# The turn from attention to the MLP in an encoder layer: the last heads' store by another queue, blocks begun a row sooner, a product emitted ahead of casts

## The chip, the cores and the metric

The kernel runs on one core of one Trainium2 chip. TensorE (PE) multiplies matrices, VectorE (DVE), ScalarE (ACT) and GpSimd (POOL) work on vectors, and SyncE (SP) issues most of the DMAs. The metric is the device time of one execution in microseconds (us), as the median of the runs.

## What is computed

One encoder layer on a sequence of 2048 tokens with 1024 features, in float32: a mixer of two groups of eight heads, and a squared-ReLU MLP. Both sub-layers have an RMS norm and a scale, shift and gate drawn from a vector c.

```python
h = rmsnorm(x, g_norm1) * (1.0 + sc1) + sh1
q_sb, k_sb, v_sb, q_ca, k_ca, v_ca = split(h @ w_in)
o_sb = stick_breaking_attention(q_sb, k_sb, v_sb)            # 8 heads, causal
o_ca = chunked_relpos_attention(norm(q_ca), norm(k_ca), v_ca, rel_bias)
x = x + gt1 * (concat(o_sb, o_ca) @ w_o)                     # output projection
h = rmsnorm(x, g_norm2) * (1.0 + sc2) + sh2
x = x + gt2 * (square(relu(h @ w1)) @ w2)                    # MLP, 4096 hidden
```

## The kernel before

**Numbers in two parts.** A float32 operand is split into a rounded part and a remainder (`split`, line 141: ScalarE casts the rounded part, VectorE or GpSimd subtracts to get the remainder, "low part" below). A product of two such operands is three matmuls (`mm3`): high by high, high by low, low by high.

**Four blocks of tokens, worked from the last to the first.** The sequence (stored reversed) is cut into four blocks g of 512 tokens. The heads are walked for g = 2 and 3, then 1, then 0, and the output projection of a block is filled in between the attention matmuls of the next. The last head pair of block 0 is thus the end of the attention. `keep` (line 798) splits the finished output o of a pair of heads into the tile os, subtracting on GpSimd, and stores it in scr_m. The choice of the queue for that store is one line (802): ScalarE's for the very last unit, GpSimd's for the other late pairs of block 0, else SyncE's.

**The turn.** When the attention is over, five of the eight rows of block 1's output projection are still left or in work (`left`, the matmuls named po; weights ow; residuals xr and txr). `row` (line 2114) emits a row to its end and the first matmul of the next one, which is where the next row's weight and residual loads are emitted. Between the rows the code emits loads and work of the MLP (`steps[0].fetch` loads the mixer's outputs of block 0, opm; `some(k, n)` emits piece n of block k, below).

Then comes a list of steps, which the loop in line 2150 emits one by one: each iteration first prepares operands of steps ahead (as many as eight tiles allow), then emits the jobs due at that step, then runs the step. The first eight are `Mixed` (line 1992): the output projection of block 0, one row each (matmuls pso; the weights still resident are ow, the others wo; residuals cxr), in the order of rows 5, 6, 7, 0 to 4. After them come the `First` steps (line 1587): the first dense layer of the MLP for the half mb = 1 of the tokens, that is blocks 2 and 3 of scr_x, by a scheme of seven products of halves instead of eight, in the order 1, 5, 6, 3, 7, 2, 4. Product 1 has a PSUM bank ps of its own; when it is done, ScalarE copies that bank to seed the bank ps_s of product 6 (lines 1643 to 1645), which products 7 and 4 go on with. The weights of products 1 and 5 are split into a tile of their own (opr) before the step; those of 6, 3, 7, 2 and 4 (opw) go into the eight buffers that held opm.

**The right-hand blocks.** The seven products need seven combinations of the normed activations, in four blocks k of 128 features (`right_blocks`, line 1503). Piece 0 loads four tiles y of scr_x (named ty for k = 0, cy for k = 1 to 3); piece 1 multiplies them by the norm's factor r on VectorE, scales and shifts them on ScalarE and casts the first three high parts; pieces 2 and 3 make the low parts, the differences and the other high parts h, going to and fro between VectorE and ScalarE. The second to fourth blocks are emitted in pieces beside the Mixed steps (`pieces`, line 2143). This half's blocks are what the change calls the second half's.

**What sets the order.** Each engine runs its instructions in the order in which the code emits them (`Ordered`, line 34; in the profile all such instructions have line 42). So a SyncE DMA that waits holds up all DMAs behind it. The DMAs of SyncE and ScalarE together take eight counters of landings in turn (DMAHW0 to DMAHW7), and GpSimd's take others (DMASW): a DMA that gets a counter waits until the DMA that had it eight places earlier has landed.

Of the kernel before, what the change touches and what calls it, by code (L numbers as in the profile page):

```python
# [24 lines left out]
KT = D // P  # L25
# [54 lines left out]
def encoder_kernel(ctx, tc, xs, c, g1, g2, w_in, w_first, w_rest, gqk, bias, w_o, w1, w2, w_ada, b_ada, out):  # L80
    nc = tc.nc
    act, dve, pool, sp = nc.scalar, nc.vector, nc.gpsimd, nc.sync
# [58 lines left out]
    def split(hi, lo, src, lo_eng=None):  # L141
        act.copy(hi, src)
        (lo_eng or dve).tensor_tensor(lo, src, hi.bitcast(F32), op=ALU.subtract)
# [100 lines left out]
    if True:  # L244
# [251 lines left out]
        act, dve, pool = (Ordered(tc, e) for e in (act, dve, pool))  # L496
# [161 lines left out]
        sp = osp  # L658
# [78 lines left out]
    if True:  # L737
# [7 lines left out]
        sp = nc.sync  # L745
# [28 lines left out]
        def finish(u):  # L774
            r = (u.h % 2) * HD
            q = HD - r
            if u.h % 2 == 0:
                pend["o", u.g] = op.tile([P, TB], F32, tag="o", name=f"o{u.nm}")
            o = pend["o", u.g]
            tmp = op.tile([P, TB], F32, tag="otmp", name=f"otmp{u.nm}")  # L780
            rows = slice(r, r + HD)
            act.copy(tmp[rows, :], u.acc[q : q + HD, :])

            def rest():
                act.copy(o[rows, :], u.acc[rows, :])
                soon.append(add)

            def add():
                pool.tensor_tensor(o[rows, :], o[rows, :], tmp[rows, :], op=ALU.add)
                if u.h % 2:  # L790
                    wait({3: 5, 0: 2}.get(u.g, 3), lambda: (urgent if u.g > 1 else heavy).append(lambda: keep(u, o)))

            urgent.append(rest)
# [4 lines left out]
        def keep(u, o):  # L798

            os = fp.tile([P, 2, TB], F32R, tag="st", name=f"os{u.nm}")  # L800
            split(os[:, 0, :], os[:, 1, :], o, pool)
            q = act if u is units[-1] else pool if u.ca and u.g == 0 else sp
            q.dma_start(scr_m[u.g, u.ca * 4 + u.h // 2], os.bitcast(F32))
            if u.ca and u.h == NH - 1 and u.g > 0:
                filler.append(Filler(outproj, u.g))
# [434 lines left out]
        units = []  # L1240
# [70 lines left out]
        def force(f):  # L1311

            got = next(f.gen, None)
            if callable(got):
                got()
            return None if got is None else callable(got)
# [41 lines left out]
        for i in range(len(steps) + LAG):  # L1358
# [31 lines left out]
            n = len(urgent) + len(heavy)  # L1390
# [4 lines left out]
            if i + 1 < len(steps):  # L1395
                u, st = steps[i + 1]
# [8 lines left out]
    sp = osp  # L1405
# [21 lines left out]
    if True:  # L1427
# [610 lines left out]
        for mb in (1, 0):  # L2038
# [22 lines left out]
            if mb:  # L2061
                norm2(1, begin + 18)
                norm2(0, begin + 48)
                for k in range(HK):
                    begins = end + 6 * k
                    pieces = right_blocks(0, k, kept if k % 2 else temp)
# [41 lines left out]
        def some(k, *ns):  # L2108
            for n in ns:
                blocks[k][n]()  # L2110
# [3 lines left out]
        def row():  # L2114

            while force(left) is False:
                pass
            while len(stores) > 2:
                stores.pop(0)()
            return force(left)  # L2120

        steps[0].fetch(0, KT // 2)
        row()
        row()
        some(0, 0)
        steps[0].fetch(KT // 2, KT - 2)
        row()
        some(0, 1)
        steps[0].fetch(KT - 2, KT)
        row()  # L2130
        some(0, 2)
        some(1, 0)
        while row() is not None:
            pass
        while stores:
# [4 lines left out]
            del resident[n]  # L2140
        for m in range(LEFT):
            steps[m].load()
        pieces = ((0, 3), (1, 1)), ((1, 2), (2, 0)), ((1, 3), (2, 1)), ((2, 2), (3, 0)), ((2, 3), (3, 1)), ((3, 2),), ((3, 3),)
        for n, now in enumerate(pieces):
            for k, m in now:
                at(n, lambda k=k, m=m: some(k, m))
# [1 line left out]
        ahead = iter(steps[1:])  # L2148
        nxt = next(ahead)
        for n, s in enumerate(steps):  # L2150
            while nxt is not None and ready - used + nxt.tiles <= 8 and nxt.ready():
                nxt.prepare()
                ready += nxt.tiles
                nxt = next(ahead, None)
            for m in (0, 1) if n == 0 else (n + 1,):
                if m < KT:
                    steps[m].load_row()
            for job in jobs.get(n, ()):
                job()
            if n == KT - 1:  # L2160
                firsts = spare.tile([P, 2, 2, TB], F32R, tag="r8", name="opr")
                steps[KT].prepare(firsts[:, 0])
                steps[KT].fetch(0)
                steps[KT + 1].prepare(firsts[:, 1])
                for m in range(1, 4):
                    steps[KT].fetch(m)
            s.run()
            used += s.frees
            later.tick()
        later.flush()  # L2170
# [42 lines left out]
```

## Time and profile before

| | us |
|---|---|
| median of 3 runs | 2512.6 |
| the runs | 2511.39 to 2512.66 |
| the profiled execution | 2509.76 |
| its span in the profile | 2508.1 |
| TensorE busy | 2497.6 |
| VectorE busy | 2028.4 |
| ScalarE busy | 1527.0 |
| GpSimd busy | 788.5 |

The turn lies at about 1266 to 1354 us of the span. In the rows of the profile a name like po<-fx,ow says that the instruction writes po and reads fx and ow; x96 is a count; "SPq" and "ACTq" are DMAs issued by SyncE and ScalarE. Bracketed text says how long the engine was idle before the instruction and what is thought to have ended that. Matmul durations overlap, since TensorE is pipelined. The granted TensorE clock was 0.999 over the run.

### The profile page before, as it was taken

The page shows a single profiled execution, that of the slowest core. Times are in us where ns is not written, and L with a number is a line of the kernel's source. Part 1 is how long each engine was busy: PE and PEld are TensorE (multiplying, and loading weights), DVE is VectorE, ACT ScalarE, POOL GpSimd, SP SyncE. Part 2 cuts the span into 40 slices and gives each one's busy share as a digit, 9 for nine tenths or more (in the row PEclk, how much of TensorE's full clock was granted, in tenths as well). Part 3 has the DMA queues.
Part 4 walks back from the last instruction along what each step waited for, and adds up shares of the span by engine and source line. Part 5 has one row for each costly group of instructions (what it writes and reads, how often), then busy time and mean ns, then how long its engine had stood idle before and what let it go on. Part 6 is the DMA issues. An engine that isn't in the chain of part 4 may idle for free.

```text
span 2508.1 us, 39516 instructions
## 1 busy us (share of the span) xinstructions
PE 2497.6 (100%) x12364; PEld 2094.6 (84%) x12364; DVE 2028.4 (81%) x3572; ACT 1527.0 (61%) x2928; POOL 788.5 (31%) x1174
## 2 busy tenths in 40 slices
PE   9999999999999999999999999999999999999999
PEld 8888888888888888888887888888888888888887
DVE  7656776897789888999868777779877759799998
ACT  6333434778876687666755555567555546577765
POOL 4330154777776677776720000000000000010100
PEclk9999999999999999999999999999999999999999
DMA  9879978789888788866786878996998996988982
GB/s 359 331 297 362 356 274 290 231 262 310 268 262 263 235 249 269 271 193 214 220 327 243 299 284 304 333 355 196 326 326 269 316 365 260 319 248 282 305 279 84
DMA packets 296114, 704.71 MB, mean 281 GB/s; under 512 B 32096, under 2 KB 88672, under 8 KB 284256
## 3 DMA queue, kind: packets, MB, share of 16 engines
q1 hardware_dynamic: 287552, 684.22, 79.1%
q0 software_dynamic: 6768, 13.11, 2.9%
q10 hardware_dynamic: 1584, 4.85, 0.5%
q8 instruction: 98, 1.61, 0.3%
q14 instruction: 112, 0.92, 0.1%
HBM read 473.99 MB, written 228.07 MB: 280 GB/s over the span
## 4 chain that ended last, share of the span: by engine, by line
PE 93%; DVE 3%; ACT 1%; DMA 1%; issue 1%; POOL 0%; SPq 0%; DVEq 0%; ACTq 0%; POOLq 0%
PE ps L42 29%; PE ps_s L42 17%; PE pt L42 11%; PE acc L42 7%; PE wt L42 7%; PE pf L42 6%; PE z L42 5%; PE po L42 4%; PE pq L42 3%; PE cz L42 2%; PE ct L42 1%; DMA opm<-scr_m 1%; PE px L42 1%; DVE h L42 0%; DVE p L42 0%
## 5 line engine op out<-in xcount | busy, mean ns | idle before, releaser
L42 ACT CAST wth<-wt 128x512 fp32r<-128x512 f32 (+3 forms) x544 | 257.8, 484 | 173.3 <-PE wt L42 160.7
L42 PE MATMUL ps<-h,opw 128*128 128x512 f32 x1512 | 358.6, 389 | 0.0
L42 POOL TENSOR_TENSOR b<-p 128x512 f32<-128x512 f32 (+1 forms) x320 | 292.5, 914 | 153.2 <-DVE p L42 94.3
L42 DVE TENSOR_TENSOR wtl<-wt,wth 128x512 fp32r<-128x512 f32 (+3 forms) x544 | 291.3, 547 | 60.4 <-ACT wth L42 56.0
L42 PEld LDWEIGHTS ps<-h,opw 128*128 128x128 f32 x1512 | 283.6, 188 | 58.9
L42 PE MATMUL pt<-w,ht 128*128 128x512 f32 x1248 | 288.0, 391 | 0.0
L42 PE MATMUL ps_s<-h,opw 128*128 128x512 f32 x1152 | 277.8, 390 | 1.0 <-ACT ps_s L42 1.0
L42 PEld LDWEIGHTS pt<-w,ht 128*128 128x128 f32 x1248 | 232.9, 188 | 47.5
L42 DVE TENSOR_TENSOR_SCAN p<-z,p,zero 128x512 f32<-128x512 f32 x192 | 245.2, 1279 | 18.6 <-ACT z L42 14.8
L42 PEld LDWEIGHTS ps_s<-h,opw 128*128 128x128 f32 x1152 | 215.6, 188 | 47.6 <-ACT ps_s L42 1.4
L42 ACT CAST opr<-r 128x512 fp32r<-128x512 f32 x280 | 174.3, 623 | 118.2 <-PE ps L42 66.4
L42 PE MATMUL acc<-wth,v 128*128 128x512 f32 (+3 forms) x544 | 221.3, 410 | 0.0
L42 PE MATMUL ps<-opr,ol 128*128 128x512 f32 x960 | 220.3, 389 | 0.0
L42 PEld LDWEIGHTS ps<-opr,ol 128*128 128x128 f32 x960 | 180.1, 188 | 37.8 <-DVE opr L42 0.4
L42 ACT ACTIVATE z<-z 128x512 f32<-128x512 f32 (+1 forms) x320 | 166.6, 521 | 52.7 <-PE z L42 49.9
L42 DVE TENSOR_TENSOR opr<-r,opr 128x512 fp32r<-128x512 f32 x280 | 185.5, 683 | 13.8 <-ACT opr L42 12.7
L42 PE MATMUL acc<-wtl,v 128*128 128x512 f32 (+3 forms) x544 | 185.6, 347 | 0.0
L42 PE MATMUL z<-k,q 128*128 128x512 f32 (+3 forms) x640 | 182.8, 367 | 0.7 <-DVE p L42 0.7
L42 POOL DMA_DIRECT2D scr_x<-txu x12 | 10.4, 868 | 544.2 <-DMA scr_x<-txo 314.9
L42 PE MATMUL ps<-oph,opv 128*128 128x512 f32 x768 | 174.9, 389 | 0.2 <-DVE txo L42 0.2
L42 PE MATMUL wt<-ident,b 128*128 128x128 f32 x1088 | 170.7, 272 | 0.4 <-DVE p L42 0.4
L42 PEld LDWEIGHTS ps<-oph,opv 128*128 128x128 f32 x768 | 144.1, 188 | 30.5 <-DVE txo L42 0.6
(238 smaller groups left out, 5064.7 us busy)
## 6 DMA issues: line engine op xcount, KB each, us to landing
r<-scr_hid SPq DMA_DIRECT2D x80, 512.0 KB, 7.5
q<-scr_q SPq DMA_DIRECT2D x128, 256.0 KB, 5.3
w<-in_w_dram SPq DMA_DIRECT2D x64, 512.0 KB, 5.8
k<-scr_k SPq DMA_DIRECT2D x240, 128.0 KB, 4.5
v<-scr_v SPq DMA_DIRECT2D x120, 256.0 KB, 4.3
wa<-in_w_ada_dram SPq DMA_DIRECT2D x48, 512.0 KB, 6.1
ow<-scr_wo SPq DMA_DIRECT2D x24, 1024.0 KB, 5.7
l<-scr_t SPq DMA_DIRECT2D x20, 1024.0 KB, 8.6
```

The lines of the kernel that those rows point to most:

```text
L42: return lambda *x, **y: self.tc.keep_in_program_order(f(*x, **y))
```

## The change

Three edits. The store of the last head pair goes by GpSimd's queue, as those of the other late pairs of block 0 do. At the turn every piece of a right-hand block is emitted a row sooner: the loads of block 0 after the first row that is left instead of the second, and so on, so that two pieces more are emitted within the rows of block 1 and the list beside the Mixed steps begins at what was its second entry. And the first `First` step is emitted before the operands of the steps ahead are prepared (`if n == KT: s.run()`, KT is 8), not after.

```diff
-            q = act if u is units[-1] else pool if u.ca and u.g == 0 else sp
+            q = pool if u.ca and u.g == 0 else sp
...
         steps[0].fetch(0, KT // 2)
         row()
+        some(0, 0)
         row()
-        some(0, 0)
         steps[0].fetch(KT // 2, KT - 2)
+        some(0, 1)
         row()
-        some(0, 1)
         steps[0].fetch(KT - 2, KT)
-        row()
         some(0, 2)
         some(1, 0)
+        row()
+        some(0, 3)
+        some(1, 1)
         while row() is not None:
             pass
...
-        pieces = ((0, 3), (1, 1)), ((1, 2), (2, 0)), ((1, 3), (2, 1)), ((2, 2), (3, 0)), ((2, 3), (3, 1)), ((3, 2),), ((3, 3),)
+        pieces = ((1, 2), (2, 0)), ((1, 3), (2, 1)), ((2, 2), (3, 0)), ((2, 3), (3, 1)), ((3, 2),), ((3, 3),)
...
         for n, s in enumerate(steps):
+            if n == KT:
+                s.run()
             while nxt is not None and ready - used + nxt.tiles <= 8 and nxt.ready():
                 nxt.prepare()
...
-            s.run()
+            if n != KT:
+                s.run()
```

SyncE's queue at the turn, before: the numbers behind a name tell one row or part of it (ow_7 is the weight of row 7, opm_4 the output of head pair 4), and the waits are in brackets.

```order
L42 DMA ow_6_16972<-scr_wo_236 128x2048 [waits DMAHW5_49,PE_49]
L42 DMA txr_5_16974<-in_xs_dram 128x512 [waits DMAHW6_49,Pool_49]
L42 DMA ow_7_17002<-scr_wo_237 128x2048 [waits DMAHW7_49,PE_49]
L42 DMA txr_6_17004<-in_xs_dram 128x512 [waits DMAHW0_49]
L42 DMA ty_0_11_17008<-scr_x_0_216 128x512 [waits DMAHW1_49]
L42 DMA ty_0_12_17010<-scr_x_0_208 128x512 [waits DMAHW2_49]
L42 DMA ty_0_21_17012<-scr_x_4_220 128x512 [waits DMAHW3_49]
L42 DMA ty_0_22_17014<-scr_x_4_212 128x512 [waits DMAHW4_49]
L42 DMA opm_4_17016<-scr_m_4_164 128x1024 [waits DMAHW5_49,DMASW0_49]
```

The counter DMAHW0 that txr_6 waits for is the one that ScalarE's store of the last heads has taken. The same place after the change:

```order
L42 DMA ow_6_16972<-scr_wo_236 128x2048 [waits DMAHW4_49,PE_49]
L42 DMA txr_5_16974<-in_xs_dram 128x512 [waits DMAHW5_49,Pool_49]
L42 DMA ty_0_11_16978<-scr_x_0_216 128x512 [waits DMAHW6_49]
L42 DMA ty_0_12_16980<-scr_x_0_208 128x512 [waits DMAHW7_49]
L42 DMA ty_0_21_16982<-scr_x_4_220 128x512 [waits DMAHW0_49]
L42 DMA ty_0_22_16984<-scr_x_4_212 128x512 [waits DMAHW1_49]
L42 DMA ow_7_17010<-scr_wo_237 128x2048 [waits DMAHW2_49,PE_49]
L42 DMA txr_6_17012<-in_xs_dram 128x512 [waits DMAHW3_49]
L42 DMA opm_4_17016<-scr_m_4_164 128x1024 [waits DMAHW4_49,DMASW0_49]
```

The four loads of ty have moved ahead of ow_7 and txr_6. The counters are one lower, since ScalarE's store takes none; opm_7 now waits for GpSimd's counter DMASW3 instead.

ScalarE's queue at the first dense products, before (opr and opw are the high parts of the weights; ps_0_1_s is the bank ps_s):

```order
L42 CAST opr<-ts_0_1_5_17492 128x512 [waits DVE_49]
L42 CAST opw_0_6_17528<-ts_0_1_6_17496 128x512 [waits DMAHW1_49,DVE_49,PE_49]
L42 CAST opw_0_3_17531<-ts_0_1_3_17498 128x512 [waits DMAHW2_49,DVE_49,PE_49]
L42 CAST opw_0_7_17534<-w_1_0_17445 128x512 [waits DMAHW4_49,DVE_49,PE_49]
L42 CAST opw_0_2_17537<-w_1_0_17445 128x512 [waits PE_49]
L42 CAST opw_0_4_17540<-w_1_0_17445 128x512 [waits DMAHW5_49,PE_49]
L42 COPY ps_0_1_s<-ps_0_1_17543 128x512 [waits PE_49]
```

The copy stands last here, behind the five casts. The same place after the change:

```order
L42 CAST opr<-ts_0_1_5_17492 128x512 [waits DVE_49]
L42 COPY ps_0_1_s<-ps_0_1_17528 128x512 [waits PE_49]
L42 CAST opw_0_6_17543<-ts_0_1_6_17496 128x512 [waits DMAHW0_49,DVE_49]
L42 CAST opw_0_3_17546<-ts_0_1_3_17498 128x512 [waits DMAHW1_49,DVE_49]
L42 CAST opw_0_7_17549<-w_1_0_17455 128x512 [waits DMAHW3_49,DVE_49]
L42 CAST opw_0_2_17552<-w_1_0_17455 128x512
L42 CAST opw_0_4_17555<-w_1_0_17455 128x512 [waits DMAHW4_49]
```

The copy that seeds ps_s has moved ahead of the five casts. On VectorE each block's products, differences and low parts stand one residual (txr or cxr) sooner than before. On TensorE the order of the matmuls is the same.

## The prediction

> **What bounds the kernel now.** I read the page first, the engines' busy times (its part 1).
>
> ```profile
> PE 2497.6 (100%) x12364; PEld 2094.6 (84%) x12364; DVE 2028.4 (81%) x3572; ACT 1527.0 (61%) x2928; POOL 788.5 (31%) x1174
> ```
>
> TensorE is busy in 2497.6 of 2508.1 us. So the change can win only time in which TensorE stands still around the turn, and that has to be measured in that stage. The next view is TensorE's timeline there: start, time, instruction, count, and in brackets the idle time before it.
>
> ```profile
> 1266.80 22.00 PE L42 MATMUL po<-fx,ow 128*128 128x512 f32 x96
> 1288.64 16.73 PE L42 MATMUL pso<-opm,ow 128*128 128x512 f32 x72
> 1305.20 27.36 PE L42 MATMUL pso<-opm,wo 128*128 128x512 f32 x120
> 1332.40 0.61 PE L42 MATMUL ps<-h,opr 128*128 128x512 f32 x2
> 1333.20 5.28 PE L42 MATMUL ps<-h,opr 128*128 128x512 f32 x22 [0.18 <-DVE opr L42]
> 1339.44 3.06 PE L42 MATMUL ps_s<-h,opw 128*128 128x512 f32 x12 [0.96 <-ACT ps_s L42]
> ...
> 1345.19 3.02 PE L42 MATMUL ps_s<-h,opw 128*128 128x512 f32 x12
> ...
> 1350.78 2.92 PE L42 MATMUL ps_s<-h,opw 128*128 128x512 f32 x12
> 1353.54 5.60 PE L42 MATMUL ps<-h,opw 128*128 128x512 f32 x24
> 1358.98 2.88 PE L42 MATMUL ps_s<-h,opw 128*128 128x512 f32 x12
> ```
>
> The durations hold a pipeline's drain, so I count from start to start. The last two rows give the pace without waits: 24 matmuls in 5.44 us, 0.2267 us each. Against that pace, the 96 po matmuls took 21.84 for 21.76 us (0.08 lost); the 72 pso matmuls on ow 16.56 for 16.32 (0.24); the 120 on wo 27.20 for 27.20 (nothing); the first two matmuls of the first dense product 0.80 for 0.45 (0.35); from there to ps_s 6.24 for 4.99 (1.25); the four products from 1339.44 to 1350.78 took 11.34 for 10.88 (0.46), the next one lost 0.04. In all **2.42 us**: that is all the turn can give back, less than 0.1% of the kernel.
>
> Next, who holds those matmuls up. ScalarE's timeline:
>
> ```profile
> 1274.04 0.33 ACTq L42 DMA_DIRECT2D scr_m<-os  x1
> ...
> 1333.78 0.62 ACT L42 CAST opr<-ts 128x512 fp32r<-128x512 f32 x1 [2.10 <-DVE ts L42]
> 1335.81 1.35 ACT L42 CAST opw<-ts 128x512 fp32r<-128x512 f32 x2 [1.41 <-PE ps L42]
> 1337.14 1.66 ACT L42 CAST opw<-w 128x512 fp32r<-128x512 f32 x3
> 1338.82 0.57 ACT L42 COPY ps_s<-ps 128x512 f32<-128x512 f32 x1
> ...
> 1344.56 0.58 ACT L42 COPY cp<-ps_s 128x512 f32<-128x512 f32 x1
> ```
>
> VectorE's:
>
> ```profile
> 1283.67 0.69 DVE L42 TENSOR_TENSOR ty<-ty,r 128x512 f32<-128x512 f32 x1 [4.91 <-DMA ty<-scr_x]
> ...
> 1330.43 1.46 DVE L42 TENSOR_TENSOR h<-cy,h 128x512 fp32r<-128x512 f32 x2
> 1331.80 0.74 DVE L42 SCALAR_TENSOR_TENSOR cxr<-pso,mod,cxr 128x512 f32<-128x512 f32 x1
> ...
> 1335.04 0.69 DVE L42 TENSOR_TENSOR ts<-ts,w 128x512 f32<-128x512 f32 x1
> ```
>
> ps_s may start only when ScalarE has copied the first product into that bank (1338.82 + 0.57 = 1339.39; it starts at 1339.44). The copy stood behind five casts of opw, and these behind the difference ts that VectorE wrote from 1335.04 to 1335.73 (the bracket names PE, but the cast at 1335.81 reads that tile). VectorE came to it late because the blocks h kept it until 1330.43 + 1.46 = 1331.89. From its first product on ty at 1283.67 the four blocks take 48.2 us, handed to and fro between the two engines. TensorE waits for none of it until 1332. Why they begin at 1283.67 is read from SyncE's queue and its waits:
>
> ```profile
> 1266.42 0.38 SPq L42 DMA_DIRECT2D txr<-in_xs_dram  x1
> 1272.51 0.32 SPq L42 DMA_DIRECT2D ow<-scr_wo  x1
> 1279.67 0.33 SPq L42 DMA_DIRECT2D txr<-in_xs_dram  x1
> 1280.05 1.85 SPq L42 DMA_DIRECT2D ty<-scr_x  x4
> ...
> 1284.14 1.36 SPq L42 DMA_DIRECT2D opm<-scr_m  x2
> ...
> 1287.20 3.48 SPq L42 DMA_DIRECT2D cy<-scr_x  x4
> ...
> 1295.48 0.33 SPq L42 DMA_DIRECT2D wo<-scr_wo  x1
> ...
> 1321.72 0.81 SPq L42 DMA_DIRECT2D w<-in_w_dram  x2
> ```
>
> ```profile
> SPq L42 <- DMA scr_m<-os: 6.8, 1, 6.8
> ```
>
> The loads ty stand behind ow_7 (1272.51) and txr_6 (1279.67), and txr_6 waited 6.8 us for the store scr_m<-os that ScalarE's queue had issued at 1274.04: the two use the same counter of landings, as the rows in the section on the change show.
>
> **The change part by part.** *The store by GpSimd's queue.* It takes one issue from ScalarE (0.33 us, ahead of a long idle time, worth nothing) and gives GpSimd one. It still waits for GpSimd's own subtraction; the rows are that subtraction and the landing of an earlier store from that queue:
>
> ```profile
> 1272.71 1.29 POOL L42 TENSOR_TENSOR os<-o,os 128x512 fp32r<-128x512 f32 x1 [0.73 <-ACT os L42]
> ```
>
> ```profile
> DMA to landing us min/median/max: 9.3/9.3/9.3
> ```
>
> The subtraction ends at 1274.00. Issued by ScalarE, the store landed just before txr_6 went out, at about 1279.6, some 5.5 us after its issue. The earlier one from GpSimd took 9.3 us, so I set the bounds of the landing at 1279.6 and 1274.3 + 9.3 = 1283.6, and take 1281, nearer to the first, since that row is for the same 0.5 MB at the same time. Nothing waits behind the issue on GpSimd. Wherever it lands, the store no longer stops txr_6, ty and opm_4 to opm_6, only opm_7 and what SyncE has behind that. The Trainium skill ("DMA: Bandwidth & Descriptors", Specifications) puts the first byte of a GpSimd transfer at about 1 us and of a SyncE or ScalarE one at about 0.6; by it the store lands 0.4 us later and the sum stays. No run here shows that difference by itself.
>
> opm_7 is the second of the pair at 1284.14, whose issues end at 1285.50, and the 0.24 us on the pso matmuls are the wait for it. If the store lands at 1281, opm_7 goes out some 4 us sooner; at 1283.6, still over 1 us. **Gain 0.2**, bounds 0 and 0.24.
>
> *Blocks a row sooner.* ty now follows txr_5, at 1266.8 instead of 1280.05, and its issues (1.85 us) end by 1268.7. Its landing is bounded by 3.6 us (1283.67 - 1280.05) and the 9.3 us above; so VectorE's first product comes between 1270.4 and 1276.1. The transfers queued ahead of it speak for the late end: I take 1276, 7.7 us sooner. The issue of cy at 1287.20 comes to stand behind opm_7, at about 1282, 5 us sooner. So the blocks end between 5 and 7.7 us sooner, at 1324 to 1327. What is then late is the weight w of the first product, issued as a pair at 1321.72:
>
> ```profile
> DMA to landing us min/median/max: 5.4/5.9/6.4
> ```
>
> Its second half lands by 1321.72 + 0.81 + 6.4 = 1328.9, as before. Cast 0.62, low part, difference, cast, low part at 0.6 to 0.7 each: both operands stand at about 1332. The first product needs its own from 1332.15 (1332.40 less 0.24), the second from 1334.9. So the 0.35 us goes; 0.1 may stay. **Gain 0.35**, bounds 0 (the blocks end as late as now) and 0.35.
>
> *First product ahead of the casts.* The copy that seeds ps_s now stands before the five opw casts and waits at the head of ScalarE's queue for the first product, with those casts, VectorE's low parts and the third product behind it. The product ends at 1332.15 + 12 x 0.2267 = 1334.87, with its drain at 1335.0; copy 0.57, first cast 0.62, low part 0.69 and the hand-overs: 1337.1. The third product starts at 1337.6 and needs the low part with its third matmul, at 1338.05. So the second product covers the new wait with 0.9 us to spare; beyond that cover each 0.1 us would cost 0.1. **Gain 1.25**, bounds 0.6 (cast and low part both uncovered) and 1.25. Of the 0.46 after it, the product at 1345.19 began when the copy at 1344.56 had ended; that copy stood behind casts of the next weight, whose load follows VectorE's last residual on SyncE, now sooner. I take **0.3** of it, bounds 0 and 0.46.
>
> Sum: 0.2 + 0.35 + 1.25 + 0.3 = 2.1 us, bounds 0.6 and 2.42. The profiled execution took 2509.76 us with a span of 2508.1: after it 2507.7 and 2506.0. The median of the runs shown, 2512.6, lies 2.8 above that execution; they reach from 2511.39 to 2512.66. On their scale: 2512.6 - 2.1 = **2510.5 us**. From 1353 on the order of instructions is as before, and all should follow 2.1 us sooner.
>
> **The rivals.** *A: the loads brought forward make ow_7 late.* ty's four, 1 MB, now stand before ow_7, and the store runs beside it. Rows: ow_7's landing, and the rate where the transfers are dense (last column, GB/s).
>
> ```profile
> DMA to landing us min/median/max: 5.9/5.9/5.9
> ```
>
> ```profile
> 1282.00:1304.00 22.00, 22.00 (x97) 17.93 (x97) 16.97 (x27) 12.31 (x19) 0.00 (x0) 1.00 1.01 380
> ```
>
> ow_7 landed at 1272.51 + 5.9 = 1278.4, and po_7 needs it at 1288.64 - 5.44 = 1283.2: 4.8 us to spare. At 380 GB/s 1 MB takes 2.8 us and the 0.5 MB store 1.4: 0.6 is left, more if a part of ty moves before ow_7 is issued. It decides below some 330 GB/s; at 250 ow_7 would be 1.5 us late, giving 2512.0. The Trainium skill ("DMA: Bandwidth & Descriptors", Issuing engines are not separate DMA queues) says that transfers run on the same 16 engines whoever starts them, and another issuer saves only the time of issue. By this rule no byte moves faster and the 0.33 us of issue is all that the new queue wins. The trace speaks against it as far as the wait goes: the 6.8 us were spent in SyncE's queue, not in moving bytes.
>
> *B: the blocks come no sooner,* because ty waits for memory that the mixer's tiles still hold. Then VectorE is as late as now; the copy, moved ahead, wins its 1.25 and the rest stays: 2511.35. Against it: txr_5, of the same pool of tiles, went out at 1266.42.
>
> *C: wo_0 comes late, and the kernel is slower.* SyncE now has cy_2's four loads ahead of wo_0, and before those a store of po_7's residual, which VectorE makes only after its products on cy_1, whose loads stand behind opm_7, which waits for GpSimd's store. wo_0 was issued at 1295.48, and landed so much later:
>
> ```profile
> DMA to landing us min/median/max: 8.5/8.5/8.5
> ```
>
> The pso matmuls on wo would start at 1304.96, so with 8.5 us it must go out by 1296.4. With every row at its worst: store landed at 1283.6, cy's four issues 3.5, landing 8.5, the last product and the residual 1.4, then six issues of about 0.4: 1299.4, landing at 1307.9, 2.9 late, net 0.8 slower: 2513.4. It outweighs the gain from a lateness of 2.1 us on. Against it: with the store at 1281 and a landing of 6 us, the least that leaves cy any queue, the same sum gives 1294.3, hardly later than TensorE frees the buffer (1288.4 + 5.44 = 1293.8), and the transfers that stood ahead of wo_0 have by then had 5 us more.
>
> **How the numbers follow.** Forecast 0.70, A 0.10, B 0.10, C 0.07, 0.03 for anything else. The range: downwards the whole 2.42 and the 1.3 by which the three runs spread, 2512.6 - 3.7, so 2508.9; upwards A and B are inside, and of C, which gives 2513.4, I leave out the upper part: 2512.8. A measurement of this kernel can tell about 0.2%, 5.0 us, from no change. No case reaches that: a turn without any loss gives 2.42, C costs less than 1. So same 0.95, faster 0.03, slower 0.02.
>
> **What would show it.** Right: ty issued before 1269; the blocks done before 1328; the pso matmuls ending, and the first dense product beginning, at about 1332.15 without a gap; the copy into ps_s before the opw casts, ended by 1335.7; ps_s at 1337.6; the product that begins at 1353.54 now near 1351.4. Wrong: idle time before po_7 (A), ty issued at 1279 as now (B), a gap before the pso matmuls on wo (C), or ps_s waiting for opw, so that the new order of ScalarE's queue takes back what it gave.

## The result, and the profile after

The changed kernel takes **2507.51 us** (median of 21 runs, 2506.35 to 2509.09) against 2511.97 us before (median of 21 runs, 2509.98 to 2514.06). The ratio is 0.9983, 95% interval 0.9977 to 0.9989: the medians lie 4.46 us apart, and by the interval the gain is between 2.8 and 5.8. The forecast of 2510.5 us was too high, and its range, which began at 2508.9, does not hold the median. The profiled execution of after took 2507.11 us, span 2505.4, so it lies 2.7 us of span below the profiled execution of before.

The turn itself went as forecast. TensorE's timeline of after, from the last output products of the first kind on (start, time, instruction, count, idle time before it in brackets):

```profile
1266.95 22.00 PE L42 MATMUL po<-fx,ow 128*128 128x512 f32 x96
1288.80 16.48 PE L42 MATMUL pso<-opm,ow 128*128 128x512 f32 x72
1305.12 27.36 PE L42 MATMUL pso<-opm,wo 128*128 128x512 f32 x120
1332.32 5.60 PE L42 MATMUL ps<-h,opr 128*128 128x512 f32 x24
1337.76 2.88 PE L42 MATMUL ps_s<-h,opw 128*128 128x512 f32 x12
...
1351.36 5.60 PE L42 MATMUL ps<-h,opw 128*128 128x512 f32 x24
```

No row has a bracket. From the first of the 96 po matmuls to the product of 24 it is 84.41 us here and 86.74 before: 2.33 us won, where the forecast said 2.1, and that product starts at 1351.36, where it said 1351.4. SyncE's queue, its wait for the store, and GpSimd's issue of that store with its landing (from a view each):

```profile
1267.03 1.98 SPq L42 DMA_DIRECT2D ty<-scr_x  x4
...
1272.67 0.32 SPq L42 DMA_DIRECT2D ow<-scr_wo  x1
...
1277.63 4.69 SPq L42 DMA_DIRECT2D opm<-scr_m  x2
...
1295.60 0.38 SPq L42 DMA_DIRECT2D wo<-scr_wo  x1
```

```profile
SPq L42 <- DMA scr_m<-os: 3.8, 1, 3.8
```

```profile
1274.47 0.58 POOL L42 DMA_DIRECT2D scr_m<-os  x1 [0.30 <-POOL os L42]
```

```profile
DMA to landing us min/median/max: 7.5/7.5/7.5
```

The four ty loads left at 1267.03 instead of 1280.05. The store landed at 1274.47 + 7.52 = 1281.99, a microsecond later than I took and inside its bounds. SyncE still waits 3.8 us for it, but now only opm_7 (the second issue of the pair at 1277.63) and what follows it stand behind that wait. ow_7, issued at 1272.67, took 9.1 us and landed 1.6 us before po_7 needed it at 1288.80 - 5.44 = 1283.36; wo_0, issued at 1295.60, took 8.3 us and landed 1.3 us before 1305.12. So neither rival A nor C happened. A was farther off than its sum said (0.6 us to spare), C was nearer: wo_0 went out 1.3 us after the 1294.3 of its milder sum. VectorE and ScalarE:

```profile
1276.41 2.51 DVE L42 TENSOR_TENSOR ty<-ty,r 128x512 f32<-128x512 f32 x4 [2.98 <-DMA ty<-scr_x]
...
1323.07 1.46 DVE L42 TENSOR_TENSOR h<-cy,h 128x512 fp32r<-128x512 f32 x2
```

```profile
1335.23 0.57 ACT L42 COPY ps_s<-ps 128x512 f32<-128x512 f32 x1 [5.55 <-PE ps L42]
1335.72 1.14 ACT L42 CAST opw<-ts 128x512 fp32r<-128x512 f32 x2
```

VectorE's first block product starts at 1276.41 (I had said 1276), the last ends at 1324.53 (1324 to 1327), and the seed copy comes before the opw casts and ends at 1335.80 (by 1335.7).

So 2.33 us of the span's 2.7 lie in the turn, but the medians are 4.46 apart. Two questions are left: which edit does it, and why the sum was too small.

### The profile page after: what moved, and what is told of

It is laid out like the page before. It is cut to its first block, busy times and chain, and to the rows that moved or that the text cites. A ratio compares the mean times of both kernels' runs of the same rounds, so it can differ in the third digit from the quotient of the medians.

```text
span 2505.4 us, 39519 instructions
## 1 busy us (share of the span) xinstructions
PE 2495.8 (100%) x12364; PEld 2095.3 (84%) x12364; DVE 2028.2 (81%) x3572; ACT 1527.0 (61%) x2928; POOL 789.6 (32%) x1175
## 4 chain that ended last, share of the span: by engine, by line
PE 97%; DVE 2%; ACT 1%; issue 0%; DMA 0%; POOL 0%; SPq 0%; DVEq 0%; ACTq 0%; POOLq 0%
PE ps L42 29%; PE ps_s L42 17%; PE pt L42 11%; PE acc L42 8%; PE wt L42 7%; PE pf L42 6%; PE po L42 5%; PE z L42 5%; PE pq L42 3%; PE cz L42 2%; PE pso L42 2%; PE ct L42 1%; PE px L42 1%; DVE p L42 0%; DVE opr L42 0%
```

## How the losses are counted

For every run below I took the starts of all 512 wide matmuls and added up what each step from one to the next had above 0.2267 us (steps above by less than 0.02 us, and four later steps that have narrower matmuls in between in every profile, left out). "Turn" is what lies between the start of the 96 po matmuls and 1360 us, "later" all after that. The profiles of the kernel before and of kernels with ScalarE's store, in us ("store" is the time from ScalarE's issue to landing; "opm" the losses among the pso matmuls on ow, which wait for the loads opm; "slow" a stretch of matmuls at 0.427 us behind such a wait; "cp" the losses after the seed, at the next ps_s products):

| profile | time | store | opm | slow | first product | seed | cp | turn | later |
|---|---|---|---|---|---|---|---|---|---|
| before, the profile of the prediction | 2509.76 | 5.61 | 0.21 | 0 | 0.45 | 1.24 | 0.24 | 2.13 | 1.69 |
| e0_same | 2510.11 | 6.51 | 1.28 | 0 | 0.23 | 1.22 | 0.36 | 3.08 | 2.22 |
| e0b_same | 2512.87 | 7.67 | 2.59 | 0 | 0.40 | 1.21 | 0.11 | 4.32 | 2.56 |
| e0c_same | 2509.98 | 6.13 | 0.80 | 0 | 0.36 | 1.23 | 0.21 | 2.61 | 1.46 |
| e0d_same | 2509.33 | 5.71 | 0.62 | 0 | 0.03 | 1.23 | 0.62 | 2.49 | 1.08 |
| mean of these five | 2510.41 | 6.33 | 1.10 | 0 | 0.29 | 1.23 | 0.31 | 2.93 | 1.80 |
| e3_product | 2509.56 | 5.58 | 0.37 | 0 | 0.18 | 0 | 1.47 | 2.03 | 2.21 |
| e3b_product | 2509.88 | 5.46 | 0.36 | 0 | 0.39 | 0 | 1.33 | 2.07 | 1.60 |
| e3c_product | 2511.01 | 7.72 | 2.34 | 1.59 | 0 | 0 | 0 | 3.93 | 1.77 |
| e3d_product | 2511.29 | 7.33 | 2.13 | 1.71 | 0 | 0 | 0.52 | 4.36 | 1.60 |

The table's 2.13 for the first row is the prediction's 2.42 without the smallest steps and the 0.06 us that every profile here loses at the start of the po matmuls. The six profiles of kernels with the store on GpSimd's queue (after, after_again, e1_store, e4_store_rows, e5_store_product, e7_shift) lost nothing more in the turn; later they lost 1.11, 1.43, 1.09, 2.47, 2.28 and 2.07, mean 1.74. Ahead of the turn the two groups do not differ: the 96 po matmuls start at 1266.57 on the mean of the five profiles of before, and at 1266.57 on the mean of these six.

## The experiments

**The kernel before again (e0_same, e0b_same, e0c_same, e0d_same).** No edit.

> The kernel before, unchanged, for a second profile and for what a comparison of a kernel with itself gives. Theory T (the turn: all that was won was lost at the turn, and the profiled execution of before happened to lose less there than most): ratio 1.000, and if this execution is one of the slower ones, the stretch from the first po of the 96 to the product after 1350 is longer than 86.74 us by about as much as the execution is longer than 2509.8. Theory L (later: the rest was won after the turn, in losses that another spacing of DMAs and matmuls takes away): the turn takes about 86.7 us as before, and the extra time stands in matmul gaps after 1353. Theory P (the profiled execution and the others differ by something before the turn, as the loads at the start): the extra time stands before 1266.

> The kernel before, one more look, to see how its losses vary between executions. So far two: 3.9 and 5.3 us of TensorE's time from the first output product on, 2.1 and 3.1 of them in the turn (the wait for opm_7 0.2 and 1.3). Theory V (the forecast was short because it was summed on an execution that happened to lose little: the losses of before reach from 3.9 to some 6 us with a mean near 5): 4 to 6 us in this look, opm_7's wait 0.2 to 1.3, losses after 1353 1.5 to 2.5. Rival W (before the turn the changed kernel is faster too): losses here about 3.9 as in the first look, and the last head's end later than the 1266 to 1267 of the changed kernel.

> The kernel before, another look, as the last. Theory V: 4 to 6 us lost from the first output product on, 2.1 to 3.1 of it in the turn. Rival W: about 3.9, and the start of the first output product later than 1267.5.

> The kernel before, a last look, as the two others. Theory V: 4 to 6 us lost from the first output product on, 2.1 to 3.1 of it in the turn. Rival W: about 3.9, and the start of the first output product later than 1267.5.

e0_same: 2510.11 us, ratio 0.9996 (0.9988 to 1.0005). The profiles are in the table. The turn lost 2.1 to 4.3 us, and the part that varies most is the wait for opm. The worst is e0b_same. Its rows of TensorE, and the landing of ScalarE's store:

```profile
1288.69 4.42 PE L42 MATMUL pso<-opm,ow 128*128 128x512 f32 x18
1294.69 0.97 PE L42 MATMUL pso<-opm,ow 128*128 128x512 f32 x3 [1.58 <-DMA opm<-scr_m]
1295.94 11.87 PE L42 MATMUL pso<-opm,ow 128*128 128x512 f32 x51 [0.28 <-DMA opm<-scr_m]
```

```profile
DMA to landing us min/median/max: 7.7/7.7/7.7
```

The store took 7.7 us where the profile of the prediction had 5.6, the queue behind it went out 2.1 us later, and the pso matmuls stood still for opm. Over the five profiles the loss at opm rises with the store's flight without an exception. So theory V holds, as far as five profiles go, and theory T with it: the profile I summed on had the smallest loss of the turn, since its store flew shortest. From the first output product on the five lost 3.9, 5.4, 6.9, 4.1 and 3.6 us, which is a wider spread than the 4 to 6 that I gave V. Rival W falls, and theory P: in e0b_same, e0c_same and e0d_same the 96 po matmuls start at 1266.85, 1266.84 and 1266.65, in after at 1266.95; in e0_same they start sooner, at 1265.73.

**The store alone (e1_store).**

```
-            q = act if u is units[-1] else pool if u.ca and u.g == 0 else sp
+            q = pool if u.ca and u.g == 0 else sp
```

> The store by GpSimd's queue alone. With it SyncE no longer stops at txr_6, ty goes out right behind ow_7 at about 1273.5, VectorE starts at about 1279.5 instead of 1283.7 and ends the blocks about 4 us sooner, at 1327.5 to 1328; the five casts then end before the first product, the copy for ps_s starts with the product's end. Theory T: the turn takes 84.4 to 84.9 us in the trace (2.33 won by all three edits), and the time is that of the changed kernel, about 4.4 us below before. Theory L: about 2.2 us below before, unless the extra hangs on this edit.

2506.85 us, ratio 0.9986 (0.9977 to 0.9995): this one line has the whole gain, as far as the intervals can tell. The turn takes 84.41 us (1350.60 - 1266.19), as in after. SyncE, ScalarE and TensorE:

```profile
1272.28 0.68 SPq L42 DMA_DIRECT2D txr<-in_xs_dram  x1
1273.01 3.50 SPq L42 DMA_DIRECT2D ty<-scr_x  x4
```

```profile
1332.71 1.35 ACT L42 CAST opw<-ts 128x512 fp32r<-128x512 f32 x2 [1.41 <-DVE ts L42]
1334.04 1.67 ACT L42 CAST opw<-w 128x512 fp32r<-128x512 f32 x3
1335.73 0.57 ACT L42 COPY ps_s<-ps 128x512 f32<-128x512 f32 x1
```

```profile
1331.56 5.60 PE L42 MATMUL ps<-h,opr 128*128 128x512 f32 x24
1336.99 2.88 PE L42 MATMUL ps_s<-h,opw 128*128 128x512 f32 x12
```

ty leaves at 1273.01, right behind ow_7 and txr_6. The seed copy still stands behind the five opw casts, as before, yet it ends at 1336.30 and ps_s needs it at 1336.99. The casts moved with VectorE, whose last block h starts at 1327.33 here and at 1330.43 before. The order of ScalarE's queue alone was therefore not what cost 1.25 us: it cost that only with VectorE late, and the store sets how late VectorE is. (VectorE's first block product came at 1281.95, later than the 1279.5 that I expected.)

**The rows alone (e2_rows).** The blocks, and with them the fetches, a row sooner; the first of these lines:

```
         row()
+        some(0, 0)
         row()
-        some(0, 0)
         steps[0].fetch(KT // 2, KT - 2)
...
```

> The blocks a row sooner alone, with the last store still by ScalarE's queue. The second ty load then waits for the counter that the store holds, until about 1279.7, and ow_7 stands behind it: issue at 1281.1, landing at 1287 or later, where po_7 needs it at 1283.3. Both theories: TensorE stands still for about 4 us before po_7, and VectorE has time to catch up, so the 2 us later in the turn go: the turn takes about 88.5 us, and the kernel is about 1.8 us slower than before in the trace. If it is no slower, the counter does not do what the order of instructions says.

2512.47 us, ratio 1.0006 (0.9997 to 1.0015). SyncE's queue, its wait, and TensorE:

```profile
1266.78 12.26 SPq L42 DMA_DIRECT2D ty<-scr_x  x4
1279.13 0.38 SPq L42 DMA_DIRECT2D ow<-scr_wo  x1
```

```profile
SPq L42 <- DMA scr_m<-os: 10.5, 1, 10.5
```

```profile
1266.71 16.54 PE L42 MATMUL po<-fx,ow 128*128 128x512 f32 x72
1286.54 8.44 PE L42 MATMUL po<-fx,ow 128*128 128x512 f32 x24 [3.28 <-DMA ow<-scr_wo]
1294.82 16.48 PE L42 MATMUL pso<-opm,ow 128*128 128x512 f32 x72
```

With ty ahead of ow_7, it is the second ty load that meets the store's counter: the issue of the four spreads over 12.26 us, SyncE waits 10.5 us, ow_7 goes out at 1279.13 instead of 1272.51, and po_7 waits 3.3 us for it. The 24 matmuls after that take 8.28 us instead of 5.44. In all the turn loses 6.2 us in this execution, against 2.93 on the mean before; the median is only 1.5 us above before's, which is not clear of noise. So rival A's lateness is real where ScalarE's store stays, and this edit needs the first one.

**The product ahead of the casts alone (e3_product, e3b_product, e3c_product, e3d_product).**

```
         for n, s in enumerate(steps):
+            if n == KT:
+                s.run()
...
-            s.run()
+            if n != KT:
+                s.run()
```

> The first product ahead of the casts alone. VectorE and the blocks are as late as before (last part of the blocks at about 1331.9), the wait for opm_7 (0.24) and the 0.35 in the first product stay, the 1.25 before ps_s goes and most of the 0.46 after it stays: the turn takes about 85.5 us, 1.25 less than before. Theory T: the time falls by more than the trace shows, by 1.3 to 2.5 us. Theory L: by about 1.25, unless the extra hangs on this edit.

> The first dense product ahead of the later casts, alone, once more. The forecast gave this edit 1.25 us; its first timing showed none (1.0002, interval 0.9993 to 1.0011), though its look had no loss at the seed. Theory D (the seed's loss is won, and what it wins is there in the time, only smaller than a set of 11 runs can tell): 0.8 to 1.4 us below before, turn losses 1.2 to 1.3 below the mean of before's five looks (2.7), losses after 1360 1.1 to 2.6 as in before (mean 1.8). Rival H (given back: what is won at the seed is lost again after 1360, where TensorE now runs ahead of VectorE's loads): time as before within 0.4 us, losses after 1360 2.2 to 3.5. Rival M (the wait for opm_7 is larger in this kernel): opm_7's part above 1.5.

> The same, a look. Theory D: losses from the first output product to 1360 0.5 to 2.6 with nothing at the seed, after 1360 1.1 to 2.6. Rival H: after 1360 2.2 to 3.5. Rival M: opm_7's part above 1.5.

> The same, a second look. Theory D: losses from the first output product to 1360 0.5 to 2.6 with nothing at the seed, after 1360 1.1 to 2.6. Rival H: after 1360 2.2 to 3.5. Rival M: opm_7's part above 1.5.

2511.35 us, ratio 1.0002 (0.9993 to 1.0011); again 2510.74, ratio 1.0001 (0.9992 to 1.0010). In all four profiles the loss at the seed is gone, yet on the mean the turn loses 3.10 us, against 2.93 before. TensorE and ScalarE in e3_product, then TensorE in e3b_product and in e3c_product:

```profile
1344.52 3.03 PE L42 MATMUL ps_s<-h,opw 128*128 128x512 f32 x12 [1.20 <-ACT cp L42]
```

```profile
1341.27 0.62 ACT L42 CAST opw<-w 128x512 fp32r<-128x512 f32 x1 [2.40 <-DMA w<-in_w_dram]
1343.36 0.62 ACT L42 CAST opw<-ts 128x512 fp32r<-128x512 f32 x1 [1.47 <-DVE ts L42]
1343.88 0.58 ACT L42 COPY cp<-ps_s 128x512 f32<-128x512 f32 x1
```

```profile
1341.46 2.88 PE L42 MATMUL ps<-h,opw 128*128 128x512 f32 x12
1345.40 3.03 PE L42 MATMUL ps_s<-h,opw 128*128 128x512 f32 x12 [1.06 <-ACT cp L42]
```

```profile
1293.91 0.96 PE L42 MATMUL pso<-opm,ow 128*128 128x512 f32 x3 [1.50 <-DMA opm<-scr_m]
1295.15 13.48 PE L42 MATMUL pso<-opm,ow 128*128 128x512 f32 x51 [0.28 <-DMA opm<-scr_m]
```

In e3_product and e3b_product, where little was lost at opm, the wait is one product of ps_s further on: at 1344.52 and 1345.40 it cost 1.47 and 1.33 us, for the copy cp of the bank. That copy stands behind a cast that waited for VectorE's difference ts, and this one behind a cast that waited for a load w. Counted from the start of the first dense product, cp starts after 11.83 us in e3_product (1343.88 - 1332.05) and after 12.16 in the kernel before (1344.56 - 1332.40): of the 1.25 us at the seed only 0.3 is left when TensorE comes to that copy. In e3c_product and e3d_product the store took 7.7 and 7.3 us, opm kept TensorE 2.3 and 2.1 us, and 1.6 and 1.7 more went on slow matmuls. Later losses are 1.60 to 2.21, so rival H falls as it was put: what is won at the seed is given back, but within the turn, not after 1360. M holds for two of four. Theory D's 1.25 us is not in the time. Whether the store's longer flight in those two has to do with the edit is open; nothing that the edit moves lies ahead of it.

**Pairs (e4_store_rows, e5_store_product).** The first line with each of the two other edits.

> The store by GpSimd's queue and the blocks a row sooner, without the product ahead of the casts. The store alone gave the whole gain (0.9986), so theory S (the store by itself ends the waits of the turn, and the two other edits only matter where the store is left on ScalarE's queue) expects what the store alone gave: 2506 to 2508 us, and PE's losses from the first po on near 1.2 us, none of them in the turn. Rival R (the rows cost something of their own, as the 2512.5 us of the rows alone suggest): 0.5 to 1.5 us above the store alone, with a wait before po_7 or ow_7's products.

> The store by GpSimd's queue and the first dense product ahead of the later casts, the blocks as before. Theory S: as the store alone, 2506 to 2508 us, since with the store moved no wait at the seed copy is left to be won. Rival R (the product's order is worth the seed's 1.25 us by itself): 0.5 to 1.25 us below the store alone, 2505.5 or less.

2507.63 us, ratio 0.9989 (0.9980 to 0.9998), and 2507.42 us, 0.9987 (0.9978 to 0.9996). Theory S holds: neither turn loses anything, and neither edit adds to the store. R falls for the product, which is not below 2505.5. For the rows it falls by the trace, which has no wait before po_7; the intervals alone would not tell 0.5 us.

**The later losses (e7_shift, after_again).** The changed kernel, and in e7_shift one small transfer more:

```
+        mark = dram.tile([P, 1], F32, name="mark")
+        at(KT + 2, lambda: sp.dma_start(mark, zero))
```

> The changed kernel with one more transfer, a column of 128 zeros that SyncE's queue stores at the third step after the first dense product; from there on each transfer of SyncE's queue counts on the completion counter that it had in the kernel before. The turn is as in the changed kernel. Theory C (the losses after 1353, at about 1563, 1746 and 1955, hang on which counter a transfer counts on, which moved by one when ScalarE's store took none): they come back, PE's losses after the turn rise from 1.1 to 1.7 to 2.4 us, and the time is 0.6 to 1.3 us above the changed kernel's in the same call. Theory L (VectorE and SyncE come out of the turn with more lead over PE, and so the waits of up to 0.9 us are covered): losses after the turn stay near 1.1 us, the time within 0.4 us of the changed kernel's. Theory N (they come and go between executions): either, and unlike the next run's.

> The changed kernel once more, on the same chip as the three others. All theories: 2506.5 to 2508.5 us, ratio near 0.9983. Theories C and L: PE's losses after the turn 1.0 to 1.3 us again, none at 1563, 1746 or 1955. Theory N: between 1.0 and 2.4 us, with one or another of these places among them.

2507.72 us, ratio 0.9987 (0.9978 to 0.9996), and 2507.19 us, 0.9987 (0.9978 to 0.9996). Both lost at one place where the first profile of after had lost nothing; TensorE and VectorE in e7_shift:

```profile
1954.11 3.03 PE L42 MATMUL ps_s<-h,opw 128*128 128x512 f32 x12 [0.68 <-DVE cp L42]
```

```profile
1943.81 0.69 DVE L42 TENSOR_TENSOR ts<-w,ts 128x512 f32<-128x512 f32 x1 [3.98 <-DMA scr_t<-twn]
1953.38 0.68 DVE L42 TENSOR_TENSOR cp<-ps_s,cp 128x512 f32<-128x512 f32 x1
```

VectorE waited 3.98 us for a transfer at 1943, came to cp at 1953.38, and ps_s waited for that: 0.95 us lost. In after_again the same place lost 0.32, in after nothing, in before 0.22, in e0_same 0.86. In e4_store_rows and e5_store_product, whose counters are not shifted back either, it lost 1.39 and 1.17. C falls: the loss near 1955 comes with the counters of before and without them, with those counters the losses near 1563 and 1746 did not come back, and the median of 2507.72 is only 0.5 us above after_again's, which is within the noise. L falls as well. From 1360 to 1540 the VectorE instructions stand at the same distance from TensorE, to 0.04 us, in nine profiles laid side by side (before, e0_same, e1_store, e3_product, e4_store_rows, e5_store_product, e7_shift, after, after_again), so no lead leaves the turn. N holds: later losses come and go with landings, 1.80 on the mean before and 1.74 with the store moved.

**The store's counter held by a small transfer (e8_tiny).** The kernel of e1_store, in which ScalarE also sends one column at the place of its old store (to a tile mark that is declared further up):

```
             q.dma_start(scr_m[u.g, u.ca * 4 + u.h // 2], os.bitcast(F32))
+            if u is units[-1]:
+                act.dma_start(mark, os[:, 1, 0:1].bitcast(F32))
```

> The store by GpSimd's queue alone, and ScalarE's queue sends, at the place where its store stood and after the same subtraction, one column of 128 values of that tile. So SyncE's queue meets the same completion counter in use as in the kernel before, but until a small transfer has landed, not until 0.5 MB have. Theory K (the price of ScalarE's store in the turn is that txr_6, and ty behind it, wait for its landing): txr_6 goes out about 2 us after the column's issue at some 1274, at 1276, between the 1272.3 of the store alone and the 1279.7 of before; ty's landings, VectorE's first block product and the turn's losses come between those of the two kernels, 0 to 1.5 us lost against about 0 and 2.1 to 3.1; time 2507 to 2509. Rival G (what counts is that half a megabyte leaves by another queue, whatever the counter does): txr_6 at 1272.3 and no loss, 2506.9. Rival A (any transfer of ScalarE there costs the full price): 2510 to 2511.

2515.34 us, ratio 1.0018 (1.0009 to 1.0027). SyncE's wait, the landing of the column, the landings of the column and of the store beside it in one view (the store's is the largest), SyncE's queue and TensorE:

```profile
SPq L42 <- DMA mark<-os: 11.8, 1, 11.8
```

```profile
DMA to landing us min/median/max: 10.6/10.6/10.6
```

```profile
DMA to landing us min/median/max: 10.6/10.7/10.8
```

```profile
1284.55 0.33 SPq L42 DMA_DIRECT2D txr<-in_xs_dram  x1
1284.93 1.85 SPq L42 DMA_DIRECT2D ty<-scr_x  x4
```

```profile
1293.42 0.97 PE L42 MATMUL pso<-opm,ow 128*128 128x512 f32 x3 [1.98 <-DMA opm<-scr_m]
1294.62 1.14 PE L42 MATMUL pso<-opm,ow 128*128 128x512 f32 x3 [0.23 <-DMA opm<-scr_m]
1297.21 14.84 PE L42 MATMUL pso<-opm,ow 128*128 128x512 f32 x54 [1.46 <-DMA opm<-scr_m]
```

My sizes were wrong: the column did not land in 2 us but in 10.6, no sooner than the half megabyte that was issued beside it. So the dose went the other way, and for that tells more. SyncE waited 11.8 us for 128 values, txr_6 left at 1284.55, five microseconds later than before, ty behind it, and the turn lost 7.0 us. Theory K's mechanism is shown in both directions: the counter that ScalarE's transfer holds until it lands stops SyncE's queue, with half a megabyte as with 512 bytes; taken away (e1_store) nothing is lost, held longer more is lost than before. G falls. A, a fixed price for any transfer there, falls too: the loss was not 2.1 to 3.1 but 7.0.

## Why the prediction was wrong, point by point

- **What bounds the kernel, and where the turn loses: right.** TensorE stood still only at the places named, and SyncE's wait for ScalarE's store was the root.
- **The store: mechanism right, size wrong.** "Gain 0.2, bounds 0 and 0.24" for opm_7 is the step that failed first. These bounds were the loss of one execution, taken for all that there is. Five profiles have 0.21 to 2.59, mean 1.10, and it follows the store's flight, which in the one I used was the shortest of the five (5.61 us; mean 6.33). A sign of it was on the table: that execution took 2509.76 us, 1.6 less than the fastest of the three runs.
- **Rows sooner, 0.35, and the product ahead, 1.25: won, but not by those edits.** I gave each loss to the edit that stands next to it. All hang on one chain (store, ty, VectorE's blocks, casts, copy), and the store's line alone cuts it at the root: e1_store has all four terms, e2_rows has a new stop instead, and e3_product moves the wait to the copy cp or loses more at opm. "Gain 1.25", and rival B with it, held that the edit wins this even with VectorE as late as before; e3_product shows that the copy cp then leaves 0.3 of it. The second half of the forecast, "bounds 0.6 and 1.25" for the product, speaks of a cover that e1_store does not even need.
- **"In all 2.42 us: that is all the turn can give back"** fails with the first point: on the mean of five profiles it is 2.93, at most 4.32. With 4.32 in its place the range would have begun at 2507.0. (The upper bounds of the four terms give 2.30; the 2.42 also holds 0.08 and 0.04 that no term wins.)
- **"From 1353 on ... all should follow 2.1 us sooner"** is right on the mean (1.80 and 1.74 lost later) and wrong between two single profiles: that of after lost 0.6 less there than before's, by chance.
- **What it adds up to.** 2.93 is lost in the turn before, nothing after, and 0.06 more comes later. The five profiled executions of before took 2510.41 on the mean, the six with the store moved 2507.32 (2507.11, 2507.17, 2506.26, 2508.57, 2507.14, 2507.64), so 3.1 us, of which 3.0 are placed. after_again, in its own set, has 3.3 us between the medians, 2510.51 and 2507.19. In the set of the result before's median was 2511.97, higher than the 2510.51 to 2510.95 of the later sets. The forecast missed by 3.0 us: 0.6 is its base (2512.6 from three runs, 2511.97 from 21), 0.8 is the turn (2.93 for 2.1), and the other 1.5 is what this set has above the profiles' mean, which its interval allows. What those executions lost was not seen. A store that flies as long as in e0b_same, which took 2512.87, would do it; that is argued, not shown.
- **The weighed rule.** The Trainium skill ("DMA: Bandwidth & Descriptors", Issuing engines are not separate DMA queues) would have let the new queue win only time of issue. On the bytes the runs agree: in e1_store ty's four landings took 8.2 to 9.2 us after issues at 1273, in before 3.6 to 5.7 after issues at 1280. On the time they don't, since a wait in SyncE's queue is no matter of bytes.

## What to carry to other kernels

A wait behind a transfer's landing has a spread, so take it from several executions before it becomes a term or a bound; one profile can hold its smallest value. Where several losses lie on one chain, price the chain by its first link and test each edit alone: two of the three edits here added nothing that could be measured. And ask, for each transfer, whose queue its completion counter can stop: that price is set by when the transfer lands, and here 512 bytes landed no sooner than half a megabyte.

## What the runs showed of the hardware that was not expected

**A short stop can cost twice.** In e3c_product, after TensorE had stood still for 2.3 us within 3.3, eight matmuls ran at 0.427 us instead of 0.227. The windows before, in and after that stretch (the granted clock is the third number from the right):

```profile
1293.90:1295.70 1.80, 1.51 (x5) 0.97 (x6) 1.80 (x4) 0.56 (x2) 0.00 (x0) 1.00 1.05 405
1295.70:1299.10 3.40, 3.40 (x9) 2.63 (x8) 3.32 (x6) 1.45 (x3) 0.00 (x0) 0.50 1.05 405
1299.10:1303.00 3.90, 3.90 (x18) 3.19 (x17) 2.88 (x6) 3.90 (x7) 0.00 (x0) 1.00 1.04 421
```

The clock was 0.50 for 3.4 us and whole again at once after it; it cost 1.6 us on top of the 2.3. The same stretch stands in e2_rows (12 matmuls after a stop of 3.4 us), in e8_tiny (10 after stops of 2.3, 0.5 and 1.8 us) and in e3d_product (after 2.1 us), but not in e0b_same, which stood still for 2.6 us at the same place. The Trainium skill ("TensorE: Matmul & The Clock Gate", The HAM clock gate) has the half clock follow an idle window of about 3.4 us that runs freely. The half clock agrees; that stops of 2.1 us can be enough, and stops of 2.6 us need not be, is what these runs add.

**A small transfer can be as late as a large one beside it.** The column of e8_tiny took 10.6 us while 0.5 MB from the same tile took 10.8; a store of the same 0.5 MB by ScalarE took 3.8 us in e2_rows and 5.5 to 7.7 in the others.
